# First products of three feed-forwards: 128-row matmuls split into two row halves that work for two blocks at a time

## The chip, the cores and the metric

The kernel runs on one core of a Trainium2 chip. The metric is the device time of one execution in microseconds (us), lower is better. Five engines matter: TensorE (PE, with its weight loads shown apart as PEld), VectorE (DVE), ScalarE (ACT), GpSimd (POOL), and SyncE (SP), which issues the weight transfers.

## The reference, cut to what matters

256 tokens of width 1024 pass through two layers of a first block (its feed-forward is dense in layer 0 and a mixture of eight experts in layer 1) and two layers of a second block. Three feed-forwards have their first products changed:

```python
# block 1, layer 0 (dense): x is 256 x 1024, w1 and w3 are 1024 x 2816, w2 is 2816 x 1024
f = (silu(x @ w1) * (x @ w3)) @ w2
# block 2, layers 0 and 1: w_up is 1024 x 5632, w_down is 2816 x 1024
u = centred_depthwise_conv(h @ w_up, ffn_conv_w)   # 3 taps along the tokens
u_gate, u_val = split(u, 2)
x = x + (silu(u_gate) * u_val) @ w_down
```

Everything is float32. The expert feed-forward and the mixers stay as they are.

## The kernel before

**Precision.** A product x @ w is made of three matmuls on a rounded format (fp32r): both operands are split into a high and a low part (xTh, xTl and wh, wl), and high-high, low-high and high-low are added up in PSUM. The weights are split on the chip: `_split` casts a raw piece to wh on ACT (line 152) and subtracts it from the raw piece on DVE, in some stages on POOL, to give wl (line 154).

**Weights.** All weights of the program form one list of jobs. A job is one transfer of up to 1 MB by SP's queue into a "raw" buffer, and is cut into pieces of 128 x 1024 values ("subs"). In block 2 there are two raw buffers and three slots of wh and wl; in block 1 there are four and four. `w()` hands out the next piece after `fill` has issued transfers and splits as far ahead as the slots allow. Splits are given a high priority in the order that the framework writes for each engine; that order is fixed when the program is built.

**First products.** `feat_group` makes a pair of blocks of 128 features x 256 tokens in one PSUM bank (2 KB a partition). A block takes one piece of weights: 8 row blocks of 128, times 3 matmuls of 128 rows x 128 columns over 256 tokens, 24 in all (lines 367 to 369). A group g of a feed-forward is two pairs, four blocks, of w1 and w3 or of the two halves of w_up; there are 11 groups in a feed-forward, so 44 blocks and 1056 matmuls.

**After a group.** The dense feed-forward takes SiLU of the first pair on ACT, multiplies by the second on DVE, and splits the product into `act`. In block 2 `conv` takes each block out of PSUM with one ACT instruction (line 1163) and two DVE instructions (line 1169); then SiLU on ACT, one multiplication on DVE (line 1796), and the split into `act` (lines 209 and 210).

**Second product.** `tok_parts` multiplies `act` by w2 or w_down, 128 x 128 x 512 matmuls (lines 177 to 179) into four banks: two of tag `mm` or `ex`, two of `sd`. Of the eight banks, `mm` has two, `sd` three, `at` two, `ex` one; in block 2 every third request for an `mm` bank is given the `ex` bank (`ps`, counter `n_ps`).

Of the kernel before, what the change touches and what calls it, by code (L numbers as in the profile page):

```python
# [20 lines left out]
D = 1024  # L21
# [11 lines left out]
class Net:  # L33
    def __init__(s, ctx, tc, A):
# [16 lines left out]
        s.n_dma = s.n_split = s.n_used = s.n_raw = 0  # L51

# [18 lines left out]
    # ---------------------------------------------------------------- weights  # L71
# [69 lines left out]
    def _split(s, i):  # L141
# [3 lines left out]
        for tag in ("wh", "wl"):  # L145
            if i >= s.edge_i or i % (s.HALF + s.wx[1]) < s.HALF:
                w = s.wa.tile([128, 1024], F32R, tag=tag, name=tag, bufs=s.HALF)
            else:
                w = s.wb.tile([128, 1024], F32R, tag=tag, name=tag, bufs=s.wx[1])
            r.append(w[:, :k * n].rearrange("p (k n) -> p k n", k=k))  # L150
# [8 lines left out]
    def fill(s, ahead):  # L159
# [8 lines left out]
    def w(s):  # L168
        s.fill(s.HALF + s.wx[1])
        r = s.subs[s.n_used]  # L170
        s.subs[s.n_used] = None
        s.n_used += 1
        return r
# [7 lines left out]
    # ---------------------------------------------------------------- helpers  # L181
# [12 lines left out]
    def rsqrt1(s, v, k):  # L194
        """1 / sqrt(-2 v) for one value a row."""
# [36 lines left out]
    def view(s, tag, *shape):  # L232
        """Scratch of 2 KB, two in turn for m0 and three for a0; in the first region it is cut from one tile."""
# [19 lines left out]
    # ---------------------------------------------------------------- T5 bias  # L253
# [117 lines left out]

    PL, PR = 3, 0.8
# [13 lines left out]
    # ---------------------------------------------------------------- block 1 mixer  # L386
# [95 lines left out]
    def mixer1(s, i):  # L482
# [13 lines left out]
        # cq | ckv | kr  # L496
# [146 lines left out]
    def layernorm(s, tt, n, gb, done=None):  # L643
        """Takes half n of token tile tt of x / ALPHA; the second half completes the tile."""
# [38 lines left out]
    # ---------------------------------------------------------------- block 1 feed-forward  # L683
# [28 lines left out]
    def ffn_dense(s, i, j, pp):  # L712
# [7 lines left out]
        for g in range(11):  # L720
            p1, p3 = s.fps(), s.fps()
            s.feat_group(p1, s.xTh, s.xTl)
            sil = s.tmp.tile([128, 2, 256], F32, tag="d0", name="sil")
            nc.scalar.activation(sil, p1, AF.Silu)
            s.feat_group(p3, s.xTh, s.xTl)
            nc.vector.tensor_tensor(out=sil, in0=sil, in1=p3, op=OP.mult)
            t, c = act[2 * g]
            s.split(t[:, 0, c:c + 2, :], t[:, 1, c:c + 2, :], sil)
# [257 lines left out]
    # ---------------------------------------------------------------- attention  # L986
# [912 lines left out]
```

## Time and profile before

| | us |
|---|---|
| median of 3 runs | 2842.46 |
| lowest and highest run | 2840.43, 2845.5 |
| span of the profiled execution, first to last instruction | 2840.1 |

The page gives no device time of the profiled execution apart from its span; the median of the runs lies 2.4 us above that span. Rows of the windows view give the busy time of each engine in a stretch with its number of instructions, the granted TensorE clock as a share of full speed, and how busy the transfers were. Busy shares of PE are of pipelined matmuls, whose ends are modelled, so the distance from one start to the next says more than the duration of one.

### The profile page before, as it was taken

The numbers are of one execution on the slowest core, as the hardware profiler recorded it, in microseconds if no ns is written. First come the engines' busy times: TensorE is split into PE (matmuls) and PEld (weight loads), VectorE is DVE, ScalarE is ACT, GpSimd is POOL, SyncE is SP. The second block draws the span as 40 slices with busy tenths as digits, with TensorE's granted clock in tenths as the row PEclk, the third lists the DMA queues.
The fourth block names the chain that finished last, engine by engine and source line by source line (L and its number), as shares of the span: only waits on it lengthen the run. The fifth ranks groups of instructions, "written<-read, shape, count | busy, mean of one in ns | idle before, by whom it ended". The sixth has DMA issues, their size and how long they took to land. (4 is left out here: it accounts for less than half of the span.)

```text
span 2840.1 us, 42537 instructions
## 1 busy us (share of the span) xinstructions
PE 2671.5 (94%) x16177; PEld 2330.1 (82%) x16177; DVE 2195.1 (77%) x3347; ACT 1724.0 (61%) x2643; POOL 511.4 (18%) x427
## 2 busy tenths in 40 slices
PE   8999999899999999999999999798999999799899
PEld 7988998798887878778787777577778977788897
DVE  6576654646788989889988898789777858987784
ACT  5464543456467777787777777555645535564553
POOL 3235000132400000000000000166520006651100
PEclk9999999999999999999999999898899999899999
DMA  7336555544679999999999998543144544223454
GB/s 216 119 119 197 181 180 170 157 138 137 231 255 359 351 349 357 348 351 344 364 347 352 343 355 293 185 132 91 51 135 159 188 152 135 78 64 121 148 180 161
DMA packets 350097, 610.39 MB, mean 215 GB/s; under 512 B 13626, under 2 KB 175752, under 8 KB 349888
## 3 DMA queue, kind: packets, MB, share of 16 engines
q1 hardware_dynamic: 347120, 601.34, 61.8%
q0 software_dynamic: 2768, 6.28, 0.9%
q8 instruction: 129, 2.11, 0.3%
q14 instruction: 80, 0.66, 0.1%
HBM read 606.56 MB, written 1.05 MB: 214 GB/s over the span
## 5 line engine op out<-in xcount | busy, mean ns | idle before, releaser
L152 ACT CAST wh<-raw 128x1024 fp32r<-128x1024 f32 (+3 forms) x1154 | 1186.8, 1038 | 712.3 <-PE mm L368 188.4
L154 DVE TENSOR_TENSOR wl<-raw,wh 128x1024 fp32r<-128x1024 f32 (+3 forms) x1031 | 1246.3, 1226 | 406.1 <-ACT wh L152 386.2
L367 PE MATMUL mm<-xTh,wh 128*128 128x256 f32 x1632 | 473.9, 290 | 5.3 <-DVE cT L1169 2.9
L369 PE MATMUL mm<-xTh,wl 128*128 128x256 f32 x1632 | 473.7, 290 | 3.5 <-DVE wl L154 1.7
L368 PE MATMUL mm<-xTl,wh 128*128 128x256 f32 x1632 | 471.3, 289 | 0.0
L154 POOL TENSOR_TENSOR wl<-raw,wh 128x1024 fp32r<-128x1024 f32 (+3 forms) x123 | 292.8, 2385 | 916.5 <-ACT wh L152 876.7
L178 PE MATMUL mm<-wl,xg 128*128 128x512 f32 x896 | 356.5, 398 | 1.6
L177 PE MATMUL mm<-wh,xg 128*128 128x512 f32 x896 | 352.6, 395 | 0.0
L179 PE MATMUL mm<-wh,xg 128*128 128x512 f32 x896 | 352.3, 393 | 0.0
L367 PEld LDWEIGHTS mm<-xTh,wh 128*128 128x128 f32 x1632 | 318.8, 195 | 11.3 <-DVE cT L1169 3.7
L369 PEld LDWEIGHTS mm<-xTh,wl 128*128 128x128 f32 x1632 | 318.5, 195 | 7.5 <-POOL wl L154 2.4
L368 PEld LDWEIGHTS mm<-xTl,wh 128*128 128x128 f32 x1632 | 318.3, 195 | 1.1 <-issue 0.2
L178 PEld LDWEIGHTS mm<-wl,xg 128*128 128x128 f32 x896 | 168.3, 188 | 42.8 <-DVE wl L154 7.6
L177 PEld LDWEIGHTS mm<-wh,xg 128*128 128x128 f32 x896 | 168.6, 188 | 37.7
L179 PEld LDWEIGHTS mm<-wh,xg 128*128 128x128 f32 x896 | 168.4, 188 | 36.3
L178 PE MATMUL sd<-wl,ac 128*128 128x512 f32 x448 | 176.3, 393 | 0.0
L179 PE MATMUL sd<-wh,ac 128*128 128x512 f32 x448 | 175.5, 392 | 0.0
L639 POOL DMA_DIRECT2D gb<-in_ln_ffn_g_dram x2 | 1.1, 560 | 966.1 <-DMA raw<-in_expert_w_dram 965.8
L177 PE MATMUL sd<-wh,ac 128*128 128x512 f32 x448 | 144.2, 395 | 0.0
L367 PE MATMUL ex<-xTh,wh 128*128 128x256 f32 x384 | 113.6, 296 | 4.7 <-DVE cT L1169 4.7
L369 PE MATMUL ex<-xTh,wl 128*128 128x256 f32 x384 | 112.6, 293 | 1.5 <-POOL wl L154 1.5
L368 PE MATMUL ex<-xTl,wh 128*128 128x256 f32 x384 | 112.4, 293 | 0.0
(581 smaller groups left out, 4949.4 us busy)
## 6 DMA issues: line engine op xcount, KB each, us to landing
raw<-in_expert_w_dram SPq DMA_DIRECT2D x336, 1024.0 KB, 5.7
raw<-in_w_in_dram SPq DMA_DIRECT2D x74, 1024.0 KB, 5.2
raw<-in_w_up_dram SPq DMA_DIRECT2D x44, 1024.0 KB, 5.1
raw<-in_dense_w_dram SPq DMA_DIRECT2D x33, 1024.0 KB, 5.3
raw<-in_w_down_dram SPq DMA_DIRECT2D x22, 1024.0 KB, 4.9
raw<-in_w_out_dram SPq DMA_DIRECT2D x16, 1024.0 KB, 5.0
raw<-in_w_branch_diff_dram SPq DMA_DIRECT2D x8, 1024.0 KB, 5.1
raw<-in_w_ple_gate_dram SPq DMA_DIRECT2D x8, 1024.0 KB, 5.1
```

The costliest lines, as they stand in the source:

```text
L152: s.nc.scalar.copy(r[0], raw)
L154: x = eng.tensor_tensor(out=r[1], in0=raw, in1=r[0].bitcast(F32), op=OP.subtract)
L177: mm(out, lhsT=lh, rhs=rh, start=start, stop=False)
L178: mm(out, lhsT=lh, rhs=rl, start=False, stop=False)
L179: return mm(out, lhsT=ll, rhs=rh, start=False, stop=stop)
L367: mm(o, lhsT=h[:, kk, sl], rhs=xh[:, kk, :], start=kk == 0, stop=False)
L368: mm(o, lhsT=h[:, kk, sl], rhs=xl[:, kk, :], start=False, stop=False)
L369: mm(o, lhsT=l[:, kk, sl], rhs=xh[:, kk, :], start=False, stop=kk == k - 1)
L639: s.nc.gpsimd.dma_start(gb[:, 0], row_bc(s.A[nm + "_g"], i * D, D))
```

## The change

Each 128-row matmul of the first products becomes two of 64 rows: rows 0 to 63 and rows 64 to 127 of the weights and of x. Two blocks are worked on together. In phase 0 the lower half works for the first block and the upper half for the second, each in its own PSUM bank, in turn; phase 1 does the same for the third and fourth block; in phases 2 and 3 the halves change blocks, so that each block receives its other half. Before phase 2 may start its first matmuls, a tiny POOL instruction has to have run that waits for the last matmuls of phase 0 (the same for phases 3 and 1). `feat_quad` takes four pieces of weights at once. Four banks hold two groups, and another four the next two groups; what follows a group is written after both groups of a set.

The slots of split weights are handed out by `_slot`, which adds memory of other tiles: in the dense feed-forward `Wc` and `OA` (until group 10), in block 2 from the end of the delta rule through the feed-forward `kd`, `qk` and `xv`. So there are six slots in each changed feed-forward. `fill` now splits as long as a slot is free.

```diff
+    def _slot(s, i):
+        some = [("wa", s.HALF)]
+        if s.wx[1] and i < s.edge_i:
+            some.append(("wb", s.wx[1]))
+        for key, bufs in some + [(t, 1) for t in s.ext]:
+            use = s.busy.setdefault(key, [])
+            if len(use) < bufs or use[-bufs] < s.n_used:
+                use.append(i)
+                return key
...
-        ahead = min(s.n_used + ahead, max(s.n_used + s.HALF, s.edge_i), len(s.subs))
-        while s.n_split < ahead and s.subj[s.n_split] < s.n_dma:
-            s._split(s.n_split)
+        while ahead and s.n_split < len(s.subs) and s.subj[s.n_split] < s.n_dma:
+            slot = s._slot(s.n_split)
+            if slot is None:
+                break
+            s._split(s.n_split, slot)
             s.n_split += 1
...
+    def banks(s, odd):
+        return [s.pm.tile([128, 2, 256], F32, tag=t, name=t, bufs=s.BANKS[t])
+                for t in (("at", "at", "sd", "ex") if odd else ("mm", "mm", "sd", "sd"))]
+
+    def feat_quad(s, banks, b, xh, xl):
...
+        H = (slice(0, 64), slice(64, 128))
+        ws = s.w(4)
+        k = ws[0][2]
+        P = [(kk, p) for kk in range(k) for p in range(3)]
+        done = []
+        for ph in range(4):
+            pair = (0, 1) if ph % 2 == 0 else (2, 3)
+            for kk, p in P:
+                ii = []
+                for half in range(2):
+                    q = pair[half ^ (ph >= 2) ^ b]
+                    h, l = ws[q][:2]
+                    r = H[half]
+                    ii.append(nc.tensor.matmul(banks[q][:, b], lhsT=(h, h, l)[p][r, kk, :],
+                                               rhs=(xh, xl, xh)[p][r, kk, :],
+                                               start=ph < 2 and (kk, p) == P[0], stop=ph >= 2 and (kk, p) == P[-1]))
+                    if ph >= 2 and (kk, p) == P[0]:
+                        dep(ii[-1], done[ph - 2])
+            if ph < 2:
+                d = nc.gpsimd.memset(s.mark, 0.0)
+                for x in ii:
+                    dep(d, x)
+                done.append(d)
...
-        for g in range(11):
-            us = []
-            for w in range(2):
-                ps = s.fps()
-                s.feat_group(ps, s.xTh, s.xTl)
...
+        for g0 in range(0, 11, 2):
+            gs = range(g0, min(11, g0 + 2))
+            ps = s.banks(g0 // 2 % 2)
+            for g in gs:
+                s.feat_quad(ps, g - g0, s.xTh, s.xTl)
+            for g in gs:
+                us = []
+                for w in range(2):
+                    u = s.tmp.tile([128, 2, 256], F32, tag=("d0", "l0")[w], name="u", bufs=2)
+                    s.conv(u, [p[:, g - g0] for p in ps[2 * w:2 * w + 2]], cw, 22 * w + 2 * g, 3, 44)
```

In the dense feed-forward the SiLU and the multiplication, one instruction each for a pair of blocks before, become two each, because the two blocks of a pair now lie in two banks.

## Rows read from the trace of the kernel before

**Rows 1.** Windows, the first and second products of the three feed-forwards.
```profile
core 0: us, PE busy (x) PEld busy (x) DVE busy (x) ACT busy (x) POOL busy (x), PEclk, DMA share, GB/s
312.60:438.60 126.00, 126.00 (x1058) 125.98 (x1056) 70.23 (x68) 58.58 (x67) 0.00 (x0) 1.00 0.59 189
438.60:500.00 61.40, 60.69 (x266) 49.40 (x264) 30.23 (x32) 23.27 (x24) 2.98 (x2) 1.00 0.48 155
2146.00:2268.00 122.00, 122.00 (x1019) 122.00 (x1018) 98.57 (x144) 72.67 (x106) 2.41 (x1) 1.00 0.55 182
2268.00:2332.00 64.00, 62.48 (x270) 49.87 (x269) 32.96 (x44) 26.32 (x33) 1.04 (x1) 1.00 0.49 165
2651.00:2772.00 121.00, 121.00 (x1010) 121.00 (x1010) 97.76 (x144) 72.43 (x106) 2.41 (x1) 1.00 0.56 183
```
**Rows 2.** Waits of PE, 2140 to 2340 us (total, times, longest).
```profile
PE sd L214 <- DVE h L1129: 2.2, 1, 2.2
PE mm L179 <- DVE xTl L210: 1.3, 1, 1.3
PE ex L178 <- DVE wl L154: 0.8, 1, 0.8
```
**Rows 3.** Timeline of PE and PEld within a first product (start, duration).
```profile
2179.99 0.28 PE L367 MATMUL mm<-xTh,wh 128*128 128x256 f32 x1
2179.99 0.19 PEld L368 LDWEIGHTS mm<-xTl,wh 128*128 128x128 f32 x1
2180.11 0.28 PE L368 MATMUL mm<-xTl,wh 128*128 128x256 f32 x1
2180.11 0.19 PEld L369 LDWEIGHTS mm<-xTh,wl 128*128 128x128 f32 x1
```
**Rows 4.** Timeline, 64-row matmuls of the first block's attention and their loads, halves in turn.
```profile
151.13 0.72 PE L1058 MATMUL sd<-dqk 64*128 64x128 f32 x8
...
151.13 0.53 PEld L1058 LDWEIGHTS sd<-dqk 64*128 64x128 f32 x8
```
**Rows 5.** Groups of instructions, PEld, whole span (busy, mean ns | idle before): one load.
```profile
L367 PEld LDWEIGHTS mm<-xTh,wh 128*128 128x128 f32 x1632 | 318.8, 195 | 11.3 <-DVE cT L1169 3.7 <-issue 3.5 <-ACT cqn L505 1.7
...
L1058 PEld LDWEIGHTS sd<-dqk 64*128 64x128 f32 x128 | 10.1, 189 | 3.2 <-issue 1.6
```
**Rows 6.** Timeline of PE, 128-row float32 matmuls of 128 columns.
```profile
149.89 0.61 PE L1083 MATMUL ex<-dv,wT 128*128 128x128 f32 x4
```
**Rows 7.** Timeline of PE, dense feed-forward, a block in which the steps are shorter.
```profile
436.02 0.28 PE L369 MATMUL mm<-xTh,wl 128*128 128x256 f32 x1
...
436.49 0.28 PE L367 MATMUL mm<-xTh,wh 128*128 128x256 f32 x1
...
436.96 0.28 PE L368 MATMUL mm<-xTl,wh 128*128 128x256 f32 x1
```
**Rows 8.** Timeline, the shortest matmuls of the program and their loads.
```profile
88.93 1.37 PE L296 MATMUL at<-dg,am 128*128 128x32 bf16 x48
...
88.93 1.27 PEld L296 LDWEIGHTS <-am 128*128 128x128 bf16 x48
```
**Rows 9.** Groups of instructions, DVE and ACT, 2146 to 2268 us.
```profile
L154 DVE TENSOR_TENSOR wl<-raw,wh 128x1024 fp32r<-128x1024 f32 x42 | 51.4, 1224 | 25.1 <-ACT wh L152 24.8
L152 ACT CAST wh<-raw 128x1024 fp32r<-128x1024 f32 x43 | 45.0, 1047 | 48.3 <-PE mm L368 30.5 <-PE ex L368 12.3 <-DMA raw<-in_w_up_dram 4.2
...
L1169 DVE SCALAR_TENSOR_TENSOR u<-mm,fcw,u 128x255 f32<-128x255 f32 x54 | 25.9, 479 | 0.6
...
L1163 ACT ACTIVATE u<-mm,fcw 128x256 f32<-128x256 f32 x28 | 13.2, 471 | 0.7 <-DVE u L1169 0.7
L1796 DVE TENSOR_TENSOR u<-u 128x512 f32<-128x512 f32 x10 | 6.9, 692 | 0.3
L210 DVE TENSOR_TENSOR act<-u,act 128x512 fp32r<-128x512 f32 x10 | 6.8, 681 | 0.0
```
**Rows 10.** Groups of instructions, POOL, whole span: a memset.
```profile
L1643 POOL MEMSET L<- 128x1024 f32 x4 | 4.5, 1134 | 14.3 <-DVE XP L1603 14.2
```
**Rows 11.** Transfers by line: KB each, median us to landing.
```profile
raw<-in_w_up_dram SPq DMA_DIRECT2D x44, 1024.0 KB, 5.1
raw<-in_dense_w_dram SPq DMA_DIRECT2D x33, 1024.0 KB, 5.3
```
**Rows 12.** Timeline of PE, the first matmuls of a second product.
```profile
2268.55 0.40 PE L177 MATMUL ex<-wh,act 128*128 128x512 f32 x1
2268.78 0.40 PE L178 MATMUL ex<-wl,act 128*128 128x512 f32 x1
```

More of the change, by code (lines that the diff above doesn't have):

```diff
@@ L51, in __init__ @@
         s.n_dma = s.n_split = s.n_used = s.n_raw = 0
+        s.busy, s.ext = {}, ()
+        s.mark = s.const.tile([1, 16], F32, name="mark")
     @contextmanager
@@ L139, in _dma, with _split @@
         return True
-    def _split(s, i):
+    def _slot(s, i):
[7 more added lines that the diff above has]
+                return key
+    def _split(s, i, slot):
         k0, k, n0, n = s.subs[i]
@@ L144, in _split @@
         r = []
[L145 to L149, printed above, removed]
+        if slot in ("wa", "wb"):
+            pool, bufs = (s.wa, s.HALF) if slot == "wa" else (s.wb, s.wx[1])
+            ws = [pool.tile([128, 1024], F32R, tag=tag, name=tag, bufs=bufs) for tag in ("wh", "wl")]
+        elif slot == "xv":
+            ws = [s.reg.tile([128, 1024], F32R, tag=slot, name="ww", bufs=2) for _ in range(2)]
+        else:
+            w = (s.const if slot in ("OA", "Wc") else s.reg).tile([128, 2, 1024], F32R, tag=slot, name="ww")
+            ws = [w[:, 0], w[:, 1]]
+        for w in ws:
             r.append(w[:, :k * n].rearrange("p (k n) -> p k n", k=k))
@@ L162, in fill, with w @@
             s.n_dma += 1
[L163 to L173 removed]
+        while ahead and s.n_split < len(s.subs) and s.subj[s.n_split] < s.n_dma:
[3 more added lines that the diff above has]
+            s._split(s.n_split, slot)
+            s.n_split += 1
+    def w(s, n=1):
+        s.fill(1)
+        r = s.subs[s.n_used:s.n_used + n]
+        s.subs[s.n_used:s.n_used + n] = [None] * n
+        s.n_used += n
+        return r if n > 1 else r[0]
     def mm3(s, out, lh, ll, rh, rl, start, stop):
@@ L370, in feat_group @@
                 b += 1
+    def banks(s, odd):
+        return [s.pm.tile([128, 2, 256], F32, tag=t, name=t, bufs=s.BANKS[t])
+                for t in (("at", "at", "sd", "ex") if odd else ("mm", "mm", "sd", "sd"))]
+    def feat_quad(s, banks, b, xh, xl):
+        nc = s.nc
+        D = mybir.DependencyInfo(mybir.DependencyClass.Sync, mybir.DependencyReason.DATA)
+        dep = lambda a, b: s.tc.add_manual_dep(a.ins, b.ins.name, D, reason="row halves")
+        H = (slice(0, 64), slice(64, 128))
[21 more added lines that the diff above has]
+                done.append(d)
     PL, PR = 3, 0.8
@@ L719, in ffn_dense @@
             act += [(t, c) for c in range(n)]
-        for g in range(11):
[L721 to L728, printed above, removed]
+        s.ext = ("Wc", "OA")
+        for g0 in range(0, 11, 2):
+            gs = range(g0, min(11, g0 + 2))
+            ps = s.banks(g0 // 2 % 2)
+            for g in gs:
+                if g == 10:
+                    s.ext = ()
+                s.feat_quad(ps, g - g0, s.xTh, s.xTl)
+            for g in gs:
+                sil = s.tmp.tile([128, 2, 256], F32, tag="d0", name="sil")
+                for b in range(2):
+                    nc.scalar.activation(sil[:, b], ps[b][:, g - g0], AF.Silu)
+                for b in range(2):
+                    nc.vector.tensor_tensor(out=sil[:, b], in0=sil[:, b], in1=ps[2 + b][:, g - g0], op=OP.mult)
+                t, c = act[2 * g]
+                s.split(t[:, 0, c:c + 2, :], t[:, 1, c:c + 2, :], sil)
         gb = s.ln_load("ln_ffn", i)
@@ L1224, in dnfeat @@
             u = cT[g // 4][:, 2 * g % 8:2 * g % 8 + 2, :]
-            s.conv(u, ps, cw, 2 * g, 5, 12)
+            s.conv(u, [ps[:, b] for b in range(2)], cw, 2 * g, 5, 12)
             th = s.tmp.tile([128, 2, 256], F32, tag="d0", name="th")
@@ L1264, in mix2 @@
         next(dn, None)
+        s.ext = ("kd", "qk", "xv")
         OD = s.dn_out(gzh)
@@ L1785, in ffn2 @@
             act += [(t, c) for c in range(n)]
-        for g in range(11):
-            us = []
-            for w in range(2):
-                ps = s.fps()
-                s.feat_group(ps, s.xTh, s.xTl)
-                u = s.tmp.tile([128, 2, 256], F32, tag=("d0", "l0")[w], name="u", bufs=2)
-                s.conv(u, ps, cw, 22 * w + 2 * g, 3, 44)
-                if w == 0:
-                    nc.scalar.activation(u, u, AF.Silu)
-                us.append(u)
-            nc.vector.tensor_tensor(out=us[0], in0=us[0], in1=us[1], op=OP.mult)
-            t, c = act[2 * g]
-            s.split(t[:, 0, c:c + 2, :], t[:, 1, c:c + 2, :], us[0])
+        for g0 in range(0, 11, 2):
+            gs = range(g0, min(11, g0 + 2))
+            ps = s.banks(g0 // 2 % 2)
+            for g in gs:
+                s.feat_quad(ps, g - g0, s.xTh, s.xTl)
+            for g in gs:
+                us = []
+                for w in range(2):
+                    u = s.tmp.tile([128, 2, 256], F32, tag=("d0", "l0")[w], name="u", bufs=2)
+                    s.conv(u, [p[:, g - g0] for p in ps[2 * w:2 * w + 2]], cw, 22 * w + 2 * g, 3, 44)
+                    if w == 0:
+                        nc.scalar.activation(u, u, AF.Silu)
+                    us.append(u)
+                nc.vector.tensor_tensor(out=us[0], in0=us[0], in1=us[1], op=OP.mult)
+                t, c = act[2 * g]
+                s.split(t[:, 0, c:c + 2, :], t[:, 1, c:c + 2, :], us[0])
         def xch(c):
```

6 lines of the change are left out of this document (3 added, 3 removed).

## The prediction

> **What bounds the kernel now.** I read the page first, then the windows of the changed stages, their waits, and the timeline at single matmuls. The three first products stand in the windows [rows 1]: 126.0 us busy of 126.0 in the dense feed-forward, 122.0 of 122.0 and 121.0 of 121.0 in the two of block 2, at full granted clock. The reader should see that PE is never idle there while DVE is busy for 81% of the stage in block 2 (98.57 of 122.0) and 56% in the dense one (70.23 of 126.0), and transfers for 55 to 59%. The waits of PE around and in the first of block 2's [rows 2] are three, at the stage's start and in the second product; none lies between. So these stages are as long as their matmuls' steps: 126.0/1058 = 0.1191 us in the dense one, 122.0/1019 = 0.1197 and 121.0/1010 = 0.1198 in block 2. A microsecond comes off the total only if a step becomes shorter, and only until another engine ends later.
>
> The timeline [rows 3] shows what a step is: a matmul starts 0.12 after the one before, and the load of the next weights starts together with it. A step for 512 columns takes 0.23 [rows 12], so 256 columns more cost 0.11; a step of 0.12 is that plus about 0.01. That 0.01 is what there is to win on the matmul side.
>
> **The change part by part.**
>
> *The halves.* 3 x 1056 = 3168 matmuls become 6336, in pairs that use different rows of the array. What decides everything is the step of a pair. No row shows fp32r matmuls of 64 rows. The nearest are the attention's float32 matmuls, issued in turn to the two halves and to two banks [rows 4]: eight loads lie in 0.53, one lasts 0.19 [rows 5], so the last starts 0.34 after the first, and four pairs stand 0.11 apart. A 64-row load is no shorter than a 128-row one (189 against 195 ns [rows 5]), yet two of them together step like one. I therefore take 0.112 for a pair. A warning stands beside it: whole-array float32 matmuls of 128 columns also step by 0.11 (four in 0.61, less 0.28 for the last, over three [rows 6]), so these rows show that halves overlap, not that halving is what removes the 0.01. Bounds: 0.109 below, about the 0.11 that the columns alone cost; above, no overlap at all, two steps of 0.112 = 0.224.
>
> The gain by 0.112: dense 1056 x (0.1191 - 0.112) = 7.5; block 2, 1056 x (0.1197 - 0.112) and 1056 x (0.1198 - 0.112) = 8.1 and 8.2. Together 23.8 us. By 0.109 it is 33.3.
>
> The page "TensorE: Matmul & The Clock Gate" of the Trainium skill (part 3, what overlaps and what doesn't) says that a weight load overlaps a running matmul only when the row groups differ, and gives a pack of n tiles as one matmul plus about 4 ns for each further tile. The trace agrees in part only: in rows 3 a load on the same rows already starts with the running matmul and the step is 0.12, not load plus matmul, so less is left to hide than the rule suggests. By the rule a pair would take about 0.11, an estimate from that page, and the gain would be about the same 24 to 30 us.
>
> *Four pieces of weights at once.* A quad is four phases of 24 pairs, 2.7 us each, 10.75 in all; today's group takes 11.5. There are six slots for the four in use. The next quad's first two pieces lie in the other two. Its third and fourth get the slots that phase 2 lets go 2.7 us before the quad ends, and are needed when the next phase 1 starts, 5.4 us after that release. Two splits take 1.05 on ACT and then twice 1.22 on DVE [rows 9], 3.5 us: 1.9 us to spare if both engines are free. In block 2 a raw buffer is let go by the same splits, about 0.8 us into the next quad; its next load lands 5.1 us after issue [rows 11], 2 us before its slot opens. In the dense stage there are four raw buffers. These cost nothing while this cover holds.
>
> *What follows a group.* In block 2 a group needs on DVE four subtractions of 1.224, eight of line 1169 at 0.479, 0.692 and 0.681: 10.1 us, or 9.5 with the overlap that the window shows (98.57 busy for a sum of about 104.4 over all its groups) [rows 1, 9]. That fits in 10.75, at nine tenths. But it now comes for two groups at once, 2 x 5.2 = 10.4 us at the end of every second quad, in an order fixed beforehand. If the splits released by phase 2, 8.1 us after that burst began, are written behind it, two subtractions of 1.22 and the burst's own two splits end near 10.4 + 2.4 + 1.05 + 2.4 = 16.3, against 13.4 when phase 1 needs them: 2.9 us of PE idle. If they are written first, nothing. Five sets end within each of the two stages. I take 0.5 us each, 5 us in all, as high priority speaks for the splits; the bounds are 0 and 29.
>
> In the dense stage DVE has 44% free; SiLU and multiplication in two pieces add some 0.35 us a group to ACT (two of about 0.47 for one of 0.59 by the nearest rows [rows 9]), hidden behind PE, which ends last.
>
> *Banks at the end.* Group 10 leaves by `ex` last. From the counter in the code (22 requests a feed-forward fewer), the second product of both block-2 layers asks for `ex` as its second bank, so a quarter of its first matmuls must wait for DVE to finish group 10, 5 us and what is queued. The other three banks give 12 matmuls of 0.23 [rows 12] a piece for every 9 that need not wait, and there are six slots. I take 1.5 us for each layer, 3 in all, between 0 and 10.
>
> *Marks.* 66 memsets on POOL tie phases together. Each has the 2.7 us of the phase between as cover; a far larger memset takes 1.13 [rows 10]. Nothing; without that cover up to 66 x 1.13 = 75 us.
>
> *More slots elsewhere.* Second products and the end of block 2's mixers split further ahead; the waits there are of 0.8 us [rows 2]. Nothing counted.
>
> *Sum.* 2840.1 (span) - 23.8 + 5 + 3 = 2824.3. The median of the runs is 2.4 above that span: 2826.7, said as 2826.5.
>
> **The rivals.**
>
> *The burst stalls PE (slower).* The place is the first quad after each set in block 2: splits behind the conv. It decides from (23.8 - 3)/10 = 2.1 us for each set. At the full 2.9 the time is 2842.5 - 23.8 + 29 + 3 = 2851. For it: DVE at nine tenths and bursts of 10 us. Against it: PE waits for no split within these stages today.
>
> *Halving removes nothing.* The pair steps like the whole matmul, 0.117 to 0.120. For it: in the dense stage one block in four steps by 0.117 (four steps from 436.02 to 436.49 and again to 436.96 [rows 7]) and the others by 0.120, while the columns are the same. With four slots in turn this looks like the place of the weights in memory, and both halves keep their rows' reads. The gain is then 0, the costs 0 to 3: 2842.5 to 2846, no difference that can be told.
>
> *A pair costs more than one matmul (slower).* Four instructions a pair, or halves that do not stream together in this format. At 0.13 the time is 2842.5 + 3168 x (0.13 - 0.1195) + 3 = 2879; one after the other, 2842.5 + 3168 x (0.224 - 0.1195) + 3 = 3177. Against it: 48 loads and 48 matmuls within 1.37 us [rows 8], 14 ns an instruction, and rows 4. For it: those are short runs, and the format differs. The same page (part 1) puts a sequencer that decodes in its firmware at about 62 ns a matmul, which for two would make 0.124 a pair, and 2842.5 + 3168 x (0.124 - 0.1195) + 3 = 2860 an estimate by that page; rows 8 speak against it here.
>
> **How the numbers follow.** The forecast has 0.54, all of it faster. The burst has 0.19 (0.03 faster, 0.05 within 0.2%, 0.11 slower), halving that removes nothing 0.17 (0.01, 0.10, 0.06), dearer pairs 0.10, slower. Faster by over 0.2% (5.7 us, about what a measurement of this kernel can tell from no change): 0.58; within: 0.15; slower: 0.27. The forecast's own range is 2809 (a pair at 0.109, no stall) to 2836. Taking in unchanged steps and the stalled burst, the range is 2808 to 2858; it leaves out the dear pairs and the tails of the others, under 0.2.
>
> **What would show it.** Right: starts of a pair some 0.01 apart and 0.112 from pair to pair; first products of 118 to 123 us; no wait of PE for lines 152 or 154 over 1 us inside them. Wrong: pairs at 0.117 or more, idle PE ended by wl at the third phase boundary after a conv burst, or PE waiting for POOL's mark.

## The result, and the profile after

The changed kernel takes 2981.7 us (median of four runs, 2977.9 to 2983.7) against 2842.0 for the kernel before beside it: a ratio of 1.0491, 95% interval 1.0478 to 1.0504. The forecast of 2826.5 and its range up to 2858 missed it. The profiled execution spans 2976.1 us, 136.0 more than before.

Where the 136.0 lie is read from the windows of the kernel after, cut at the first and last matmul of the three first products (length, then busy time and instructions of PE, PEld, DVE, ACT and POOL, granted clock, share of the DMA engines and GB/s, as in [rows 1]):

```profile
311.40:449.40 138.00, 133.66 (x2114) 131.47 (x2113) 65.97 (x77) 54.08 (x77) 3.32 (x24) 1.00 0.55 177
449.40:2177.20 1727.80, 1620.56 (x8487) 1361.38 (x8486) 1401.85 (x1929) 1135.04 (x1570) 254.21 (x203) 0.96 0.73 255
2177.20:2345.80 168.60, 142.05 (x2115) 137.94 (x2114) 96.03 (x146) 71.68 (x106) 2.74 (x23) 0.92 0.40 132
2345.80:2742.70 396.90, 343.51 (x2102) 296.04 (x2102) 289.06 (x573) 197.87 (x400) 156.53 (x148) 0.87 0.34 107
2742.70:2910.60 167.90, 144.36 (x2115) 140.63 (x2114) 96.62 (x147) 72.14 (x106) 2.23 (x22) 0.90 0.39 129
```

Before, the same five stretches were 126.0, 1702.2, 128.1, 376.3 and 128.4 us, with PE busy throughout in the first products [rows 1]. So the dense product lost 12.0, the two of block 2 40.5 and 39.5, and the two stretches between, which the change hardly touches, 25.6 and 20.6; the rest is 2.2 the other way. In block 2's products PE is now idle for 26.6 and 23.5 us, and its granted clock is lower too (0.92 and 0.90, from 1.00 in [rows 1]). The step is read first, since all of the gain was to come from it, then the stalls and the stretches between.

**The step.** The timeline of PE in the dense product after, at the place that answers to [rows 3]; each row is one pair:

```profile
330.03 0.29 PE L416 MATMUL sd<-xTl,wh 64*128 64x256 f32 x2
330.15 0.29 PE L416 MATMUL sd<-xTh,wl 64*128 64x256 f32 x2
330.27 0.29 PE L416 MATMUL sd<-xTh,wh 64*128 64x256 f32 x2
```

A pair starts every 0.12 us. The 24 pairs of an undisturbed phase take 2.88 in all three stages, and 44 phases make 126.7, what whole matmuls took. The two halves do run together, and nothing is saved.

**The stalls.** Waits of PE after, in the first product of layer 0 of block 2 (total, times, longest), where [rows 2] had none:

```profile
PE ex L416 <- ACT wh L169: 12.2, 5, 5.5
PE sd L416 <- ACT wh L169: 6.3, 3, 3.0
PE ex L416 <- DVE wl L171: 4.6, 5, 1.3
PE sd L416 <- DVE wl L171: 3.4, 5, 1.3
```

Most of it falls on one place: the second phase of the first quad after each set takes 8.4 to 11.0 us in place of 2.88, five times a stage; other phases, most of them of odd quads, lose 0.4 to 1.7. In the dense product the same phase takes 4.3 (the first 5.7, the last 3.8). What ACT does ahead of the second of them, in its timeline (start, duration, operation, and the idle time before it with its releaser; L169 casts a piece, L1225 and L1860 are a convolution and a SiLU):

```profile
2233.86 1.05 ACT L169 CAST wh<-raw 128x1024 fp32r<-128x1024 f32 x1 [7.60 <-PE at L416]
2234.81 0.47 ACT L1225 ACTIVATE u<-at,fcw 128x256 f32<-128x256 f32 x1
...
2241.08 0.63 ACT L1860 ACTIVATE u<-u 128x512 f32<-128x512 f32 x1 [1.13 <-DVE u L1231]
2241.61 1.98 ACT L169 CAST wh<-raw 128x1024 fp32r<-128x1024 f32 x2
```

Two things are to be seen. ACT stands 7.6 us at a cast whose slot PE has not let go, with convolutions queued behind it. And the two casts that PE needs from 2239.4 on stand at 2241.61 behind convolution work that itself waits for DVE. PE starts again at 2242.69.

A stall costs more than its wait. Two windows of PE, the phase ahead of this stall and the matmuls behind it (length, PE busy with its number of matmuls, granted clock, transfers):

```profile
2236.50:2239.40 2.90, 2.90 (x53) 1.00 0.02 6
2243.30:2250.10 6.80, 6.15 (x58) 0.50 0.76 238
```

After PE has stood idle for 3.0 and 0.8 us, its granted clock is 0.50, the lower of its two levels, for 6.8 us, and a pair starts every 0.21 us in place of 0.12. So of the 40.5 and 39.5 us that block 2's products lost, 26.6 and 23.5 are idle PE, and the other 14 and 16 go with the lower clock. In the dense product, where no wait of PE is longer than 0.6 us, the clock stays at 1.00.

**The stretches between.** Windows of the kernel after over the end of layer 0's mixer, then the same of before up to its first product (2140.8):

```profile
1980.00:2020.00 40.00, 31.02 (x128) 26.19 (x128) 36.26 (x83) 24.07 (x64) 18.65 (x20) 0.50 0.00 1
2020.00:2060.00 40.00, 39.33 (x289) 31.33 (x290) 22.91 (x75) 20.53 (x72) 10.53 (x24) 0.73 0.01 1
2060.00:2177.20 117.20, 99.21 (x715) 90.28 (x715) 76.45 (x128) 52.40 (x84) 40.12 (x23) 0.93 0.51 163
```

```profile
1980.00:2020.00 40.00, 36.63 (x268) 33.41 (x267) 37.60 (x68) 28.22 (x62) 23.03 (x20) 0.91 0.28 90
2020.00:2060.00 40.00, 37.85 (x297) 30.99 (x296) 24.78 (x82) 25.16 (x81) 15.84 (x24) 0.83 0.08 27
2060.00:2140.80 80.80, 66.96 (x487) 58.38 (x486) 64.29 (x128) 35.69 (x71) 20.39 (x21) 0.95 0.41 133
```

The columns are those of the windows above. For 80 us in which the delta rule ends, the kernel after loads next to no weights (share 0.00 and 0.01, before 0.28 and 0.08), PE does half as many matmuls in the first 40 us, at a clock of 0.50, and the tail behind it is 36.4 us longer. The DMA queue's own wait in that tail of the kernel after names what held it, a subtraction into one of the extra slots:

```profile
SPq L139 <- DVE ww L171: 154.0, 8, 112.2
```

### The profile page after: what moved, and what is told of

Read it like the earlier page. It is cut to its first block, busy times and chain, and to the rows that moved or that the text cites. A ratio compares the mean times of both kernels' runs of the same rounds, so it can differ in the third digit from the quotient of the medians.

```text
span 2976.1 us, 48945 instructions
## 1 busy us (share of the span) xinstructions
PE 2731.9 (92%) x19345; PEld 2377.5 (80%) x19345; DVE 2181.7 (73%) x3358; ACT 1719.1 (58%) x2654; POOL 522.2 (18%) x493
## 5 line engine op out<-in xcount | busy, mean ns | idle before, releaser
L169 ACT CAST wh<-raw 128x1024 fp32r<-128x1024 f32 (+2 forms) x1063 | 1088.9, 1038 | 662.0 <-PE mm L198 156.6
L171 DVE TENSOR_TENSOR wl<-raw,wh 128x1024 fp32r<-128x1024 f32 (+1 forms) x953 | 1151.3, 1230 | 421.9 <-ACT wh L169 405.2
L171 POOL TENSOR_TENSOR wl<-raw,wh 128x1024 fp32r<-128x1024 f32 (+2 forms) x110 | 264.2, 2404 | 593.7 <-ACT wh L169 549.7
L386 PE MATMUL mm<-xTh,wh 128*128 128x256 f32 x688 | 204.1, 297 | 8.5 <-DVE cT L1231 6.6
L388 PE MATMUL mm<-xTh,wl 128*128 128x256 f32 x688 | 203.9, 296 | 1.0 <-DVE wl L171 1.0
L387 PE MATMUL mm<-xTl,wh 128*128 128x256 f32 x688 | 201.8, 293 | 0.0
L198 PEld LDWEIGHTS mm<-wh,xg 128*128 128x128 f32 x896 | 168.4, 188 | 36.3
L416 PE MATMUL sd<-xTh,wh 64*128 64x256 f32 x784 | 178.8, 298 | 12.3 <-ACT wh L169 12.3
L416 PE MATMUL sd<-xTh,wl 64*128 64x256 f32 x784 | 178.0, 298 | 7.9 <-DVE wl L171 7.8
L416 PE MATMUL sd<-xTl,wh 64*128 64x256 f32 x784 | 176.7, 296 | 0.0
L386 PEld LDWEIGHTS mm<-xTh,wh 128*128 128x128 f32 x688 | 135.8, 197 | 13.5 <-DVE cT L1231 7.4
L169 ACT CAST ww<-raw 128x1024 fp32r<-128x1024 f32 (+1 forms) x91 | 92.4, 1029 | 83.8 <-DMA raw<-in_w_up_dram 19.1
```

Of the source, the lines that this page charges most:

```text
L169: s.nc.scalar.copy(r[0], raw)
L171: x = eng.tensor_tensor(out=r[1], in0=raw, in1=r[0].bitcast(F32), op=OP.subtract)
L198: return mm(out, lhsT=ll, rhs=rh, start=False, stop=stop)
L386: mm(o, lhsT=h[:, kk, sl], rhs=xh[:, kk, :], start=kk == 0, stop=False)
L387: mm(o, lhsT=h[:, kk, sl], rhs=xl[:, kk, :], start=False, stop=False)
L388: mm(o, lhsT=l[:, kk, sl], rhs=xh[:, kk, :], start=False, stop=kk == k - 1)
```

## The experiments

Times are medians; a ratio is against the kernel before on the same chip. A first product's length runs from the start of its first matmul to that of its last, plus one step of 0.12; "mixers" are the two stretches between.

| kernel | us | ratio, 95% interval | first products | mixers |
|---|---|---|---|---|
| before | 2842.0 | 1 | 126.0, 127.9, 128.2 | 1702.1, 376.4 |
| after | 2981.7 | 1.0491 (1.0478 to 1.0504) | 137.9, 168.4, 167.7 | 1728.0, 397.1 |
| e1_ext_late | 2967.4 | 1.0449 (1.0400 to 1.0499) | 138.0, 184.8, 183.6 | 1706.2, 371.3 |
| e2_oldest | 2942.7 | 1.0362 (1.0332 to 1.0392) | 128.9, 147.8, 149.3 | 1729.6, 399.9 |
| e3_whole | 2892.4 | 1.0185 (1.0155 to 1.0215) | 126.3, 130.1, 131.7 | 1730.9, 397.1 |
| e5_whole_late | 2843.1 | 1.0016 (1.0005 to 1.0027) | 126.5, 129.6, 129.9 | 1704.1, 374.8 |
| e6_single | 2868.6 | 1.0109 (1.0089 to 1.0129) | 129.9, 134.7, 134.7 | 1704.5, 377.2 |
| e7_late_oldest | 2903.9 | 1.0229 (1.0205 to 1.0254) | 128.9, 150.5, 153.5 | 1704.7, 382.2 |
| e8_bf16_low | 2842.7 | 1.0015 (1.0004 to 1.0025) | 126.6, 128.6, 128.3 | 1702.8, 377.4 |
| e9_fill_first | 2904.5 | 1.0213 (1.0184 to 1.0243) | 128.9, 151.9, 153.1 | 1702.8, 382.7 |
| e10_casts_first | 2874.7 | 1.0128 (1.0077 to 1.0179) | 128.9, 140.5, 141.4 | 1704.7, 378.1 |
| e11_hold | 2889.1 | 1.0179 (1.0128 to 1.0230) | 126.4, 129.2, 127.8 | 1730.5, 398.3 |
| e12_together | 2895.6 | 1.0192 (1.0172 to 1.0213) | 126.3, 131.3, 131.6 | 1728.8, 398.5 |
| e13_order_only | 2982.7 | 1.0499 (1.0478 to 1.0520) | 140.0, 169.5, 170.3 | 1726.3, 398.6 |
| e14_best_halves | 2847.1 | 1.0024 (1.0014 to 1.0034) | 129.9, 129.9, 130.2 | 1703.8, 374.5 |
| e15_order_all | 2947.3 | 1.0370 (1.0318 to 1.0422) | 138.5, 152.2, 152.1 | 1726.7, 397.4 |
| e16_single_only | 3019.4 | 1.0624 (1.0569 to 1.0679) | 132.1, 182.7, 181.9 | 1732.2, 405.3 |
| e17_whole_cured | 2837.3 | 0.9989 (0.9979 to 0.9999) | 126.2, 129.5, 129.4 | 1700.8, 372.5 |

### The extra slots: e1_ext_late

```
# mix2, after the delta rule
-        s.ext = ("kd", "qk", "xv")
# ffn2, before its first quad
+        s.ext = ("kd", "qk", "xv")
```

> The changed kernel, but the three slots of the delta rule's memory (kd, qk, xv) are given to the weights only when block 2's feed-forward begins, not at the end of its mixer. Theory (these slots make the mixer's tail longer, since pieces that should be split during the delta rule wait for its memory): the stretch from the dense product's end to the feed-forward of layer 0 shrinks from 1728.1 us by about 26, the one between the feed-forwards by about 21, the first products stay at 168; in all near 2981.7 - 47 = 2935. Rival (the tail is longer because the pieces are now chosen by what is free and not by their number): no change, 2975 to 2990.

The mixers fall by 21.8 and 25.8 us, 47.6 against the expected 47; with e5 against e3 it is 26.8 and 22.3 again. So the loss of the mixers is the slots' doing. The code says how: the products behind the delta rule are written after it but used to run inside it; a piece that is given `kd`, `qk` or `xv` can't be split until the delta rule is done with that memory, every later piece is behind it, and the raw buffers stay full. Windows of e1, which answer to those of after above:

```profile
1980.00:2020.00 40.00, 36.87 (x272) 34.49 (x272) 39.27 (x66) 21.26 (x41) 16.75 (x12) 0.92 0.33 102
2020.00:2060.00 40.00, 38.17 (x256) 33.81 (x256) 24.69 (x72) 28.02 (x78) 19.17 (x25) 0.74 0.13 41
```

The transfers are back. Not foreseen: the first products of block 2 grow by 16 us each; the first two phases of the first quad after each set now take 8.8 to 9.6 and 6.3 to 7.1 us. That the stage begins with other slots in turn may be why; no run shows it by itself.

### Which slot: e2_oldest

```
-            if len(use) < bufs or use[-bufs] < s.n_used:
-                use.append(i)
-                return key
+            last = use[-bufs] if len(use) >= bufs else -1
+            if last < s.n_used:
+                free.append((last, key))
+        if free:
+            key = min(free)[1] if s.age else free[0][1]   # age: in the first products
+            s.busy[key].append(i)
+            return key
```

> The changed kernel, but in the feed-forwards a piece takes the slot that was let go first, not the first free slot of a fixed list. In the changed kernel the list gives the third and fourth piece of every second quad slots that the quad before lets go only with its last phase. Theory slots: that is the stall at the second phase of every second quad; the phases of 4.3 us in the dense stage and of 8.4 to 11.0 us in block 2 become 2.9, the dense stage falls from 137.7 to about 130 and those of block 2 from 168 to about 130, in all near 2981.7 - 8 - 2 x 38 = 2898. Theory burst: in block 2 the casts stand behind the convolution's operations on ACT whatever slot they take; the dense stage falls by 8 and block 2's stay above 160, in all near 2970.

Between the two theories. The dense product falls by 9.0, every stall of its second phases gone; block 2's by 20.6 and 18.4, and stalls of 1 to 4 us in the first two phases of the second quad of four sets remain, at another quad than in the kernel after.

### Whole matmuls in the quads: e3_whole and e5_whole_late

```
-        for ph in range(4):          # pairs of 64-row halves, marks
-            pair = (0, 1) if ph % 2 == 0 else (2, 3)
...
+        for q in range(4):           # piece after piece, 128 rows
+            h, l = ws[q][:2]
+            for kk, p in P:
+                s.nc.tensor.matmul(banks[q][:, b], lhsT=(h, h, l)[p][:, kk, :], ...)
```

> The changed kernel with its quads, sets, banks and slots, but each matmul whole (128 rows) and the four pieces of a quad used one after another, without marks. If halving removes nothing from a step, steps stay at 0.120 us and nothing is lost by going back. Theory slots (halves hold four pieces until the third and fourth phase, so slots come free late): each slot is let go after a quarter of the quad, the stalls go, the first products fall to 127 to 132 us each, in all near 2981.7 - 8 - 2 x 38 = 2898. Theory burst: stalls of 5 us and more stay at the first quad after each set in block 2, whose stages stay above 160, in all near 2970.

The stalls go: 126.3, 130.1 and 131.7. Undoing the halves, with their phases and marks, is worth 89.3 us, two thirds of the loss.

e5 joins this edit with e1's:

> Whole matmuls in the quads (as in e3) and the three extra slots only from the feed-forward on (as in e1); sets of two groups, banks and the choice of slots as in the changed kernel. Theory (the loss has two parts, halves that hold four pieces, and slots that block the mixers' tails; what is left of the change costs nothing): 2892.4 - 22 - 26 = 2844, the kernel before within 5 us. Rival (with the slots given late the stalls of the first products grow, as in e1 by 16 a stage): 2860 to 2880.

2843.1, within 0.2% of before. The two causes add up to all of the loss.

### What a step costs: m1_steps and m2_widths

> A kernel that computes nothing of the reference and writes zeros: series of 48 matmuls on zeros, each with weights of its own: fp32r on all 128 rows, on two 64-row halves in turn in two banks, and on the upper half alone, for 256, 128, 64 and 512 columns; the same in bf16 for 256; whole ones with the weights in six places. Theory A (each half of the array repeats its own start-up of about 0.013 us for each matmul, both at the same time): whole, pair and half alone have the same step at each width: 0.120 at 256, about 0.067 at 128, 0.227 at 512. Theory B (a pair's step is bounded by its four instructions, and the half's own step would be shorter): the pair stays at 0.11 or more at 128 and 64 columns while whole and half alone go to 0.067 and 0.04. Theory C (the 0.013 is the load of the weights that is not hidden): whole steps differ from half-alone steps, and a pair at 512 columns beats a whole one. Places: 0.117 for some and 0.120 for others, or one value for all.

Six windows of m1, each 4.80 us long, inside the series of 256 columns (whole, pairs, upper half alone), of 128 columns (whole, pairs) and of bf16 with 256 columns (whole). The columns are those of the two windows of PE above; the count takes in matmuls that started up to 0.3 us before the window:

```profile
31.60:36.40 4.80, 4.80 (x43) 1.00 0.00 0
37.60:42.40 4.80, 4.80 (x84) 1.00 0.02 3
43.50:48.30 4.80, 4.80 (x42) 1.00 0.00 0
49.20:54.00 4.80, 4.80 (x46) 1.00 0.00 0
54.70:59.50 4.80, 4.80 (x92) 1.00 0.01 3
134.20:139.00 4.80, 4.80 (x46) 1.00 0.00 0
```

By their starts the steps are 0.120, 0.120 and 0.120 at 256 columns, 0.112 and 0.112 at 128, 0.227 for all three at 512, 0.109 in bf16. Theory A holds at 256 and 512; at 128 its 0.067 is far off: whole matmuls, pairs and halves alone all stop at 0.112. Six places of the weights gave 0.120 each, so the 0.117 of [rows 7] isn't the place as such.

> Like m1, a kernel that computes nothing of the reference: series of 48 fp32r matmuls on all 128 rows of 144, 160, 192, 224, 320, 384 and 448 columns; of 256 columns with weights of 64 columns, whole and in halves; of 256 columns with every third, then every second matmul in bf16; float32 of 256 columns, whole and in halves. If a step is the larger of a floor of 0.112 and of columns plus 0.013, the widths give 0.112 up to 224 columns (0.093 + 0.013 = 0.107 is still under the floor), then 0.147, 0.173 and 0.200. If the 0.013 is the end of the weights' load, weights of 64 columns give less than 0.120 at 256, whole or halved; if it belongs to the matmul, 0.120. If bf16 in turn with fp32r gives nothing (as e8 had it), three steps take 0.360; by the formats' own steps 0.349.

Windows of m2, again 4.80 us: 224 columns, 320 columns, 256 columns with weights of 64 columns (whole, then halves), and every third in bf16:

```profile
48.60:53.40 4.80, 4.80 (x45) 1.00 0.00 0
54.50:59.30 4.80, 4.80 (x35) 1.00 0.00 0
79.30:84.10 4.80, 4.80 (x45) 1.00 0.01 3
85.00:89.80 4.80, 4.80 (x88) 1.00 0.00 0
90.80:95.60 4.80, 4.80 (x43) 1.00 0.02 3
```

144 to 224 columns all step by 0.111 to 0.112, 320 by 0.147, 384 by 0.174 (448 by 0.2065 where 0.200 was expected). Weights of 64 columns bring 256 columns to 0.113, whole and halved alike. So what stands above the columns goes with the columns of the weights and not with their rows, and halving rows can't remove it. Float32 of 256 columns steps by 0.216, whole or per pair.

That the floor too goes with the columns of the weights, the kernel before shows in float32. Two groups of its matmuls of 64 columns, with weights of 128 columns and of 64, at full granted clock:

```profile
110.76 1.00 PE L1023 MATMUL ex<-mla,wT 128*128 128x64 f32 x8
2556.42 0.39 PE L1738 MATMUL at<-xv,qk 128*64 128x64 f32 x4
```

By their starts the first step by 0.11 us (only the second of the eight comes sooner), the others by 0.06.

### A format with a shorter step: e8_bf16_low

```
# _split, pieces of the first products, kernel before
-                w = s.wa.tile([128, 1024], F32R, ...)
+                dt = BF16 if tag == "wl" and s.low[s.subj[i]] else F32R
+                w = s.wa.tile([128, 1024], dt, ...)
# feat_group: xb is a bf16 copy of xTh
-                        mm(o, lhsT=l[:, kk, sl], rhs=xh[:, kk, :], ...)
+                        mm(o, lhsT=l[:, kk, sl], rhs=xb[:, kk, :], ...)
```

> The kernel before, with the low part of the first products' weights and a copy of the high part of x in bf16 for the third of each three matmuls (its products are rounded to bf16, the rest stays). Theory (the 0.011 us above the columns belongs to the fp32r weights of each matmul, since in the series of m1 bf16 matmuls of 256 columns step by 0.109 and fp32r ones by 0.120, whole or halved): every third step is 0.109, 3 x 352 x 0.011 = 11.6 us less, less about 2 for the copies: near 2832. Rival (the price stands at each change of format or with the matmul before): steps stay at 0.120 or grow, 2842 to 2850.

No gain: three steps take 0.360, as in m2's series with every third in bf16. In these series the 0.109 belongs to runs of bf16 alone.

### Both cures: e7_late_oldest, e9_fill_first, e10_casts_first

e7 is e1 and e2 together.

> The changed kernel with both cures, slots late and oldest slot first; sets of two groups as in the changed kernel. If the two causes add: 2942.7 - 22 - 26 = 2895, first products of block 2 at 147 to 149 us with the stalls of e2 left.

2903.9, some 9 above that sum, with the stalls of e2 left. e9 adds a line ahead of the set's convolutions:

```
                 s.feat_quad(ps, g - g0, s.xTh, s.xTl)
+            s.fill(1)
             for g in gs:
```

> e7 (halves, both cures, sets of two groups), with the splits of the next pieces asked for right after a set's matmuls and so written ahead of the set's convolutions, not behind them. Theory (what is left in e7, some 5 us a set, are casts written behind two groups' convolutions on ACT and DVE): the stages of 150 and 153 us fall towards the 135 of e6, in all 2865 to 2875. Rival (the order on ACT is decided by priority and by when a slot comes free, so that asking earlier changes nothing): 2895 to 2910.

The rival: nothing changes, and ACT's timeline shows the casts where they were. e10 forces the order (the convolutions are tied to the last split; with the oldest slot first, all four casts then come ahead of them):

```
+            with s.behind(s.pieces[0]), s.behind(s.pieces[1]):   # cast and subtraction of the last split
                 for g in gs:
```

> e9 with the order forced: in block 2 a set's convolutions stand on ACT and DVE behind the four splits asked for after its matmuls. In e9 the program asked first, but the order on ACT stayed that of e7. Theory (what is left in e7 is that order): the casts no longer wait for 15 us of convolutions, the stalls of 2 to 4 us at each second quad go, stages fall from 150 and 153 to about 135, in all near 2904 - 15 - 18 = 2871. Rival (DVE, with two groups' work and eight subtractions a set, is simply full at this rate): the stall only moves to the banks, 2890 to 2910.

2874.7, and stages of 140.5 and 141.4: the order carries 10 to 12 us a stage, some two thirds of what was expected.

### Sets of one group: e6_single and e16_single_only

```
-        for g0 in range(0, 11, 2):
-            gs = range(g0, min(11, g0 + 2))
-            ps = s.banks(g0 // 2 % 2)
+        for g0 in range(11):
+            gs = (g0,)
+            ps = s.banks(g0 % 2)
```

> Halves as in the changed kernel, with both cures (slots late, oldest slot first) and what follows a group written after each group, in sets of one. Theory (what e2 left, some 5 us at each set of block 2, are casts written behind two groups' convolutions; one group's burst of 5.2 us is over before the casts are due): stalls under 1 us a group, first products 128 to 132 us, in all 2843 to 2855, so no gain from halves, but no loss. Rival (the stalls come from the hold of four pieces in six slots whatever the burst): like e7, 2885 to 2900.

With both cures, 2868.6: stages of 134.7, 15.8 and 18.8 less than e7's, and a time between the two forecasts. The same edit by itself on the changed kernel:

> The changed kernel with one change: sets of one group, so that a group's convolutions are written and can run right after its own quad. In the changed kernel ACT stands 7.2 to 7.6 us at a cast whose slot is not yet let go, with the first group's convolutions behind it, and both groups' work then comes at once. Theory (that pile-up is the stall): block 2's first products from 168 to 135 to 145, in all 2915 to 2940. Rival (the choice of slots, unchanged here, keeps the stall): stages above 155, in all above 2955.

Worse than the changed kernel, by 14 us a stage. My theory of a pile of two groups falls: a shorter burst helped only together with the other choice of slots, given late.

### Is it the hold? e11_hold and e12_together

```
# e12: whole matmuls, pieces of a pair in turn
+        for ph in range(4):
+            for kk in range(k // 2 * (ph // 2), k // 2 * (ph // 2 + 1)):
+                for p in range(3):
+                    for q in ((0, 1), (2, 3))[ph % 2]:
+                        s.nc.tensor.matmul(banks[q][:, b], lhsT=(h, h, l)[p][:, kk, :], ...)
# e11: the loop over q stands outside those over kk and p
```

> The changed kernel with whole matmuls, but the four pieces of a quad held as its halves hold them: the first phase takes the first four row blocks of pieces 0 and 1, the second those of 2 and 3, the third and fourth the other row blocks. Theory (what costs is the hold of four pieces, not the form of the matmul): the stalls are those of the changed kernel, first products 137, 165 to 170 each in block 2, in all 2960 to 2985. Rival (matmuls of 64 rows cost the stalls themselves, by the order that they give to the other engines or by their loads): near e3, 2890 to 2910.

> The changed kernel with whole matmuls that need and let go the pieces just as its halves do: in each phase the two pieces of a pair take turns matmul by matmul, over the first four row blocks in phases one and two, the others in three and four. Unlike e11, both pieces of a pair are needed from a phase's start and held to its end. Theory hold (what stalls is that two pieces are needed at once, from slots let go at once): first products 137 and 165 to 170, in all 2960 to 2985. Theory order (the stalls come with the order of ACT and DVE that the build fixes for 64-row matmuls): block 2's stages near 130 as in e11, with at most the 1.2 us of the dense stage at each second quad, in all 2889 to 2910.

The hold is not it: e11 takes 2889.1, e12 2895.6. With the slots, sets and hold of the changed kernel, e12's whole matmuls (without marks) run in 131.3 and 131.6, and the dense product has no stall at all. What differs is ACT. Its waits over block 2's first product of layer 0, in the kernel after and then in e12:

```profile
ACT wh L169 <- PE mm L416: 32.5, 4, 10.5
ACT u L1225 <- DVE u L1231: 18.9, 10, 2.0
ACT wh L169 <- PE at L416: 15.2, 2, 7.6
ACT act L228 <- DVE u L1862: 12.6, 10, 2.3
```

```profile
ACT wh L169 <- PE mm L407: 15.2, 2, 8.8
ACT wh L169 <- DMA raw<-in_w_up_dram: 14.1, 4, 4.4
ACT ww L169 <- DMA raw<-in_w_up_dram: 11.2, 6, 2.9
ACT u L1208 <- DVE u L1214: 7.5, 5, 1.8
ACT act L228 <- DVE u L1845: 5.3, 5, 2.3
ACT wh L169 <- PE sd L407: 3.6, 3, 2.0
```

In the kernel after, ACT's casts wait 47.7 us for slots that PE has not let go, and its convolutions and splits 31.5 for DVE; in e12 it is 18.8 and 12.8. The order of each engine's queue is fixed when the kernel is built, and for pairs of 64 rows another one came out than for whole matmuls: in e12 no cast after the stage's start waits for PE longer than 2.0 us. In its last three sets two convolutions stand ahead of the set's fifth cast, the one that in the kernel after stands ahead of all eight and holds them for 7.2 to 7.6 us; e12's casts wait for transfers instead (25.3 us, 10.2 in the kernel after), which costs PE under 4 us in the stage.

### The order alone: e13_order_only and e15_order_all

e13 is e10's edit on the changed kernel itself.

> The changed kernel with nothing new but the order of block 2's first products: a set's convolutions stand on ACT and DVE behind the splits asked for right after its matmuls (as in e10); slots chosen from the fixed list and given early, as in the changed kernel. Theory order: the stalls of 5.5 to 8 us fall to the 1.2 to 2 of the dense stage, block 2's first products from 168 to 135 to 142, in all 2915 to 2935. Theory hold or slots: the stages stay above 155, in all above 2955.

Nothing: its convolutions were tied to the last split alone, which goes to a slot let go early, and the casts that matter stayed behind. e15 puts the convolutions behind all four:

```
+            s.pieces = []
+            s.fill(1)
+            with ExitStack() as e:
+                for x in s.pieces:
+                    e.enter_context(s.behind(x))
                 for g in gs:
```

> e13 mended: there the convolutions stood only behind the last of the four splits, whose slot is let go early, and the casts that the stalls wait for were free to come after. Here they stand behind all four; nothing else differs from the changed kernel. Theory order: the stalls of 5.5 to 8 us in block 2's first products fall to 1 to 2, stages from 168 to 135 to 145, in all 2915 to 2940. Rival (ACT then waits even longer for the last slot with the convolutions behind it, and the next pieces are late in turn): stages above 155, in all above 2955.

Between the two: stages fall by 16.2 and 15.6, to 152. Order and choice of slots are each worth some 16 to 21 us a stage (e2), and neither is enough.

### What halves are worth: e14_best_halves and e17_whole_cured

e14 is e6 with e10's order; e17 is e14 with e3's whole matmuls.

> Halves with everything cured at once: slots late, oldest slot first, sets of one group, and convolutions behind the splits. If no stall is left but that of each stage's start (3 us, in e5 too), halves give what whole matmuls give, since a pair steps like a whole one: first products 128 to 131 us, in all 2843 to 2850. If halves have a price of their own, some us more at each quad: 2860 to 2870, as e6. Below 2836: a pair would be shorter than a whole matmul after all.

> e14 (slots late, oldest slot first, sets of one group, convolutions behind the splits) with whole matmuls, piece after piece, in place of halves. Theory (a pair steps like a whole matmul, and with the queues in order halves have neither price nor gain): first products within 2 us of e14's 129.8, 129.8 and 130.1, in all 2840 to 2848, no difference from e14's 2847 that can be told. If halves have a price that e14 still pays, some us less: below 2840.

Windows of the three first products, of e14 and then of e17:

```profile
309.16:439.09 129.93, 129.93 (x2113) 129.88 (x2112) 67.08 (x78) 55.22 (x77) 2.23 (x22) 1.00 0.59 188
2142.93:2272.80 129.87, 128.37 (x2113) 127.73 (x2113) 97.59 (x147) 70.37 (x104) 2.69 (x23) 0.98 0.56 182
2647.35:2777.54 130.19, 128.69 (x2113) 128.06 (x2113) 97.52 (x147) 70.46 (x104) 2.23 (x22) 0.97 0.52 171
```

```profile
309.41:435.66 126.25, 126.25 (x1058) 126.25 (x1056) 72.22 (x80) 58.39 (x77) 0.00 (x0) 1.00 0.61 192
2136.45:2265.99 129.54, 128.39 (x1058) 128.04 (x1057) 98.20 (x148) 72.63 (x104) 0.22 (x1) 0.98 0.58 187
2638.49:2767.90 129.41, 128.26 (x1057) 127.91 (x1057) 98.18 (x148) 72.62 (x104) 0.00 (x0) 0.98 0.54 176
```

In block 2 halves and whole matmuls take the same to 0.8 us: no price, no gain. The dense product with halves is 3.7 longer: at its start the pieces come one at a time, one half runs alone at 0.12 a step, and its first, second and fifth phase take 5.4, 3.1 and 3.6 in place of 2.9 each. The mixers are 3.0 and 2.0 longer, for a reason not looked into. Together 9.9 us, which is the 0.35% between 1.0024 and 0.9989. So e17's time is that of its second case, a small price that e14 still pays, but not in block 2's first products; e17 is within 0.2% of before. No halved kernel beat the kernel before.

## Why the prediction was wrong

**The step of a pair** (23.8 us of gain; measured 0). The 0.112 came from [rows 4], whose matmuls are float32 of 128 columns, and those rows don't show a pair's price at 256 columns of fp32r. Float32 takes 0.216 for 256 columns (m2), so some 0.108 for 128 by the columns alone, an estimate from m2; and in fp32r every step up to 224 columns is the floor of 0.112 that m1 and m2 found, at 128 columns whole or halved. The warning beside the number, that whole matmuls of [rows 6] step like that too, was the right reading and should have decided. At 256 columns a whole matmul, a pair and a half alone are all 0.120. The rival "halving removes nothing" was right on the step; its reason, the place of the weights, was not borne out by m1.

The page "TensorE: Matmul & The Clock Gate" of the Trainium skill (section "LDWEIGHTS (loading the stationary operand)") says that a load's time goes by the columns of the weights and not by their rows; m2 agrees, since weights of 64 columns step by 0.113 and halved rows by no less than whole ones. That rule spoke against this change, and I had not weighed it. Its rule in part 3, that loads overlap a running matmul only in other rows, m1 contradicts: the upper half alone, always on the same rows, steps by 0.120 with loads of 0.19.

**What follows a group** (5 us; measured 91.9 with the dense stage, 11.9 + 40.5 + 39.5). The rival "the burst stalls PE" had the right place, the first quad after each set, and the right engines. Its size, 2.9 a set, was 5.5 to 8.1: 3.7 to 6.0 of idle PE, and 1.8 to 2.7 of matmuls at the lower clock behind it, for which the sum had no term. The idle time was larger because two of the steps under it failed. "Its third and fourth get the slots that phase 2 lets go" is wrong for every second quad: the fixed list hands them slots that only the last phase frees (e2: 9 us of the dense stage, 18 to 21 of each in block 2). And the burst was reckoned as a block of 10.4 us that starts at once; in the queue that was built it starts late, behind a cast that waits 7.6 us for a slot (e12, e15). Why the build writes the queues so for 64-row matmuls no run shows; that stays open.

**"More slots elsewhere ... Nothing counted"** (0; measured 46.2). I took more slots as more freedom. They lie in memory that other work holds to its end, and pieces are split and loaded in a fixed order (e1: 47.6 back).

**Banks at the end** (3 us): no wait of PE in the second products of block 2 is for `ex`, and the span from the last first product to the end is 65.5 us after and 66.5 before; no cost. **Marks** (nothing): right. The group of POOL after:

```profile
L422 POOL MEMSET mark<- 1x16 f32 x66 | 6.7, 101 | 476.3 <-PE mm L416 175.2 <-PE at L416 123.7 <-PE sd L416 107.1
```

0.10 us each, and no wait of PE in the first products names POOL. **A pair costs more than one matmul**: wrong, 0.120. The four instructions of a pair cost nothing at this width.

## What to carry to other kernels

Take the step of a matmul from its own number of columns and format: a narrow one sits on a floor of its weights and says nothing of a wide one, and splitting the rows leaves that floor where it is. Before counting extra buffers as free, look who holds their memory and until when, since one piece that waits for it stops every transfer queued behind. An edit to one engine's instructions can change the order that is built for the others: read in the trace what ACT waits for, and what is behind it. And a stall can cost more than its idle time: look at the granted clock behind it.

## What the chip showed that I had not expected

- An fp32r matmul of 144 to 224 columns steps by 0.111 to 0.112 us, the same as one of 128; 256 columns take 0.120, 320 0.147, 512 0.227.
- Behind stalls of 3.0 and 0.8 us PE's granted clock was 0.50 for 3.4 or 6.8 us; in block 2's products this made a third or more of the loss.
- bf16 steps by 0.109 at 256 columns, but every third one among fp32r leaves three steps at 0.360.
- In m1 PE was busy throughout, and its granted clock still fell to 0.50, the lower level, in the last series of 128 columns and stayed there through those of 64:

```profile
66.00:78.00 12.00, 12.00 (x57) 0.50 0.00 0
78.00:98.00 20.00, 20.00 (x143) 0.50 0.00 1
98.00:112.00 14.00, 14.00 (x52) 0.80 0.01 1
```

It rose again within the series of 512 columns, the third row.
